# A two-layer encoder trunk with seven-product MLPs: moving the operand sums of the MLP ramp to VectorE, and the loads and places of its second phase

## The chip, the core and the metric

One core of a Trainium2 chip runs the whole kernel in one launch. The metric is device time in microseconds (us), the median of several executions. Engines are named as the profile does: PE is TensorE (PEld its weight loads), DVE is VectorE, ACT is ScalarE, POOL is GpSimd, and SP is the engine whose one queue issues nearly every DMA here. [...]

## What is computed

The input is one sequence of 1024 tokens of width 1024. There are two layers, each a mixer (attention in the first, gated linear attention in the second) and then an MLP, both with a norm ahead and a residual:

```
def sq_relu_mlp(h, w_in, w_out):
    return jnp.square(jax.nn.relu(h @ w_in)) @ w_out

for i in range(DEPTH):                      # DEPTH = 2
    hn = rmsnorm(h, norm_mix[i])
    h = h + (attention_mixer if i == 0 else gla_mixer)(hn, ...)
    h = h + sq_relu_mlp(rmsnorm(h, norm_mlp[i]), mlp_w_in[i], mlp_w_out[i])
return rmsnorm(h, final_norm)
```

`w_in` is 1024 x 4096 and `w_out` 4096 x 1024, all in float32. Everything the change touches lies in the MLP: the step from the mixer's output projection into `h @ w_in` (here the ramp), and the step from there to `@ w_out` (here the junction).

## The kernel before

Activations are held transposed, as tiles of 128 features x 512 tokens: `h[m][half]`, m = 0 to 7. Every matrix product is made of three matmuls of 128x512 (`mm_into`, L462 to L464): each float32 operand is split into a high part, cast on ACT (L97: `xh`, `wh`, `hh`), and a low part, the remainder, subtracted on DVE (L98: `xl`, `wl`, `hl`), and the products high-high, high-low and low-high are added in PSUM.

`layer_rest` (L750) is the second half of a layer. It first projects the mixer's output, adds the residual (L799), stores the result as `hm_dram`, and sums squares for the norm. `mid_norm` (L773) turns the sums of one half of the tokens into a factor `rm`: `SumSquares.rms` splits the sums into two parts (`sqh`, `sql`) and adds over the partitions with two matmuls against a matrix of ones (L161, L162), and `newton` (L125) takes the inverse root on ACT and DVE. `normed` (L776, L778) scales an `h` tile by it in place.

The MLP uses seven products P1 to P7 in place of eight, of operands that are sums and differences of quarters of the activations. With left and right half of the tokens (second index 0 and 1) and upper and lower half of the features (tiles 0 to 3 and 4 to 7): P1 and P2 use the quarters `h[k][0]` and `h[4+k][0]`; P5 uses T1 = `h[k][1] - h[k][0]` (L822); P6 uses T2 = `h[4+k][1]` - T1 (L830, tile `t2`); P7 uses T3 = `h[4+k][1] - h[k][1]` (L836, on POOL); P3 uses B22 = `h[4+k][1]`; P4 uses T4 = `h[4+k][0]` - T2 (L832, on POOL). Each operand is four tiles, and each tile is split (`xsplit`, L768).

**Phase 1** (`mlp_in`) runs 8 groups of hidden features, 7 products each, 24 matmuls per product, in the order of the list `steps` (L582): P1, P2 of group 0 and of group 1, then P5, P6, P7, P3, P4 of group 0, the same five of group 1, then all seven of each later group. A product's PSUM banks are drained by a copy on ACT (L554, tiles `s1`, `s5`, `s2`) or an add on DVE (L557); two banks with tag a and two with tag b are in turn added to by several products (P6, P7 and P4 go on in the banks of P1, P3 in those of P5). Outputs go to `hid_dram` (L530). The drained tiles of all but the first `s1` come from the pool `hid` (L845), opened after the pools `hp` (the `h` tiles) and `scratch` have closed, so a `hid` tile lies where an `h` tile lay, and its first writer waits for the last reader of that one.

**Phase 2** (`mlp_out`) runs 4 groups x 7 products x 2. Its operands are loaded from `hid_dram` into `hst` (L601, 3 buffers of 512 KB), and split into `hh` and `hl`. Its weights go to `raw`, `raw2` (6 buffers). The residual `h` is reloaded from `hm_dram` (L868, 16 loads of 256 KB) and needed only when the first outputs are drained.

Order: the tile framework's scheduler emits each engine's instructions in program order, but for blocks in `tc.high_priority(offset=-n)`, which it puts back by n; `LATER` = 150 is that number for T3, B22 and T4. Each engine then runs its list strictly in order. All loads and stores stand in SP's one list. Pools opened after others have closed take their memory.

Of the kernel before, what the change touches and what calls it, by code (L numbers as in the profile page):

```python
# [23 lines left out]
F32 = mybir.dt.float32  # L24
F32R = mybir.dt.float32r
AF = mybir.ActivationFunctionType
ALU = mybir.AluOpType
# [4 lines left out]
P = 128  # L32
# [9 lines left out]
NCH = S // P  # L42
LEAD = 22
LAG = 3
LATER = 150


C_MIX0, C_MLP0, C_MIX1, C_MLP1, C_FIN, C_QA, C_QB, C_KA, C_KB, C_OUT, NCOL = 0, 8, 16, 24, 32, 40, 41, 42, 43, 44, 46
# [2 lines left out]
def trunk_kernel(tc, xT, wqk, wv, wo, win0, wout0, gqk, gv, gvz, gr, gate, gwo, win1, wout1, cols, rope, cmat, yT):  # L51
    nc = tc.nc

    def pool_of(stack, name, bufs=1, side=None):
        return stack.enter_context(tc.tile_pool(name=name, bufs=bufs, side=side, reuse_waits="tile"))

    with ExitStack() as top:
# [35 lines left out]
        def bank(tag):  # L93
            return psum.tile([P, HN], F32, tag=tag, name="ps_" + tag, bufs=PS_BUFS[tag])
# [27 lines left out]
        def halves(n):  # L122
            return [[None, None] for _ in range(n)]
# [14 lines left out]
        class SumSquares:  # L138
# [15 lines left out]
                split(ah, al, self.acc)  # L154
                self.acc = ah, al

            def total(self, mat, tag="c"):
                if not isinstance(self.acc, tuple):
                    self.parts()
                ps = bank(tag)  # L160
                nc.tensor.matmul(ps, mat, self.acc[0], start=True, stop=False)  # L161
                nc.tensor.matmul(ps, mat, self.acc[1], start=False, stop=True)  # L162
                return ps

            def rms(self, n, out=None):

                return newton(self.total(ones), n, out)

        def gain_split(h, g, xh, xl, k, half, sums=None):

# [337 lines left out]
        def mlp_in(win, x, hx, hid, hid_dram):  # L508
# [71 lines left out]

            rest = ("P5", "P6", "P7", "P3", "P4")
            steps = [(g, p) for g in (0, 1) for p in ("P1", "P2")] + [(g, p) for g in (0, 1) for p in rest]  # L582
            steps += [(g, p) for g in range(2, ngr) for p in ("P1", "P2") + rest]
            return steps, begin, prep, run, combine, reload

# [164 lines left out]
        def layer_rest(w, src, o, gcol, win, wout, last, ahead, begun):  # L750
# [4 lines left out]
            with ExitStack() as ph:  # L755
                env.raw = Turns((wraw, 2), (pool_of(ph, "mraw", 4), 4))
                with ExitStack() as one:
# [4 lines left out]
                    env.tmp = pool_of(scratch, "tmpr", side="right")  # L762
                    big2 = pool_of(one, "big2", 8)
                    ht = halves(KT)
                    x = [([None] * 4, [None] * 4) for _ in range(7)]
                    r = [None, None]

                    def xsplit(what, k, t, pool):  # L768
                        x[what][0][k] = pool.tile([P, HN], F32R, tag="hi", name="xh")
                        x[what][1][k] = pool.tile([P, HN], F32R, tag="lo", name="xl")  # L770
                        split(x[what][0][k], x[what][1][k], t)

                    def mid_norm(half, sums):  # L773
                        r[half] = sums.rms(D, wpool.tile([P, HN], F32, tag="ro", name="rm", bufs=2))

                    def normed(k, half):  # L776
                        t = ht[k][half]
# [7 lines left out]
                    for half in range(2):  # L785
                        sums = SumSquares(nc.vector if half else nc.gpsimd)
                        for m in range(KT):
# [7 lines left out]
                            xr = hx.tile([P, HN], F32, tag="hx", name="xr")  # L795
                            nc.sync.dma_start(out=xr, in_=src[m][:, HALF[half]])
                            ps = begun.pop(0) if begun else proj("b" if m % 4 == 0 else "a", wm, o, half)
                            h = ht[m][half] = hp.tile([P, HN], F32, name=f"h{m}_{half}")
                            nc.vector.tensor_tensor(out=h, in0=ps, in1=xr, op=ALU.add)  # L799
                            sums.add(h)  # L800
                            nc.sync.dma_start(out=hm_dram[m][:, HALF[half]], in_=h)
# [23 lines left out]
                        run(*next(ramp))  # L825
                    prep(*next(weights_ahead))
                    reload()
                    for k in range(4):
                        t2 = env.tmp.tile([P, HN], F32, tag="sq", name="t2", bufs=2)
                        nc.vector.tensor_tensor(out=t2, in0=normed(4 + k, 1), in1=ht[k][0], op=ALU.subtract)  # L830
                        xsplit(T2, k, t2, big)
                        nc.gpsimd.tensor_tensor(out=ht[4 + k][0], in0=ht[4 + k][0], in1=t2, op=ALU.subtract)  # L832
                    prep(*next(weights_ahead))
                    with tc.high_priority(offset=-LATER):
                        for k in range(4):
                            nc.gpsimd.tensor_tensor(out=ht[k][1], in0=ht[4 + k][1], in1=ht[k][1], op=ALU.subtract)  # L836
                            xsplit(T3, k, ht[k][1], big)
                        for k in range(4):
                            xsplit(B22, k, ht[4 + k][1], big)
                        scratch.close()  # L840
                        big3 = pool_of(one, "big3", 4)
                        for k in range(4):
                            xsplit(T4, k, ht[4 + k][0], big3)
                    mid.close()
# [6 lines left out]
                            begin(g + 1) if g else None  # L851
                        run(g, p)
                env.tmp = pool_of(ph, "tmp2", side="right")
                raw2 = pool_of(ph, "raw2", 6)
                hst = pool_of(ph, "hst", 3)
                hp = pool_of(ph, "hacc", side="right")
                ht = halves(KT)
                for half in range(2):
# [4 lines left out]
                begin(0)  # L863
                for st in steps[:2]:
                    load(*st)
                for row, half in ((0, 0), (0, 1), (4, 1), (4, 0)):
                    for m in range(row, row + 4):
                        nc.sync.dma_start(out=ht[m][half], in_=hm_dram[m][:, HALF[half]])  # L868
                prep(*steps[0])
                for n, st in enumerate(steps):  # L870
                    if n + 2 < len(steps):
                        load(*steps[n + 2])
                    if n + 1 < len(steps):
                        prep(*steps[n + 1])
                    if st[1:] == ("P6", 0):
                        begin(st[0] + 1)
                    run(*st)
# [375 lines left out]
```

## Time and profile before

| | |
|---|---|
| median of 3 executions | 2418.49 us (2416.34 to 2419.13) |
| the profiled execution: its own time | 2420.54 us |
| span of its records | 2418.8 us |
| PE busy | 2318.6 us (96%) |
| DVE / ACT / POOL busy | 1791.2 (74%) / 1346.6 (56%) / 365.7 (15%) us |
| mean granted clock | 0.983 |

The profile is read from PE outward. PE is busy nearly all the time, so the first question is where it is not: the 40 slices of the page show it below nine tenths in a few only. The table of waits for such a stretch says which operand ended PE's idle time, the timeline of PE shows each pause and the distance between matmul starts after it (0.23 us at the full clock, 0.43 us at half), and the timelines of DVE, ACT, POOL and SP in the same stretch say what the producer of that operand did in the meantime.

### The profile page before, as it was taken

How to read it: one execution, taken by the hardware profiler on the slowest of the kernel's cores; microseconds unless marked ns; L12 is line 12 of the kernel's file. 1: busy time of each engine (PE TensorE's matmuls, PEld its weight loads, DVE VectorE, ACT ScalarE, POOL GpSimd, SP SyncE). 2: the span in 40 equal slices, each digit the busy share in tenths (PEclk: the TensorE clock that was granted, in tenths of full speed). 3: DMA queues.
4: the chain of work that ended last, by engine and by line, in shares of the span. 5: the costliest groups of instructions: out<-in, count | busy, mean ns of one | idle time of the engine just before them, and what ended most of it. 6: DMA issues, size and time to landing. Idle time of an engine off the chain costs nothing. (4 is left out here: it accounts for less than half of the span.)

```text
span 2418.8 us, 29927 instructions
## 1 busy us (share of the span) xinstructions
PE 2318.6 (96%) x10710; PEld 1907.9 (79%) x10710; DVE 1791.2 (74%) x2488; ACT 1346.6 (56%) x2388; POOL 365.7 (15%) x283
## 2 busy tenths in 40 slices
PE   8889999999979999899999999999979999899997
PEld 6777777777868888788888889888858888788885
DVE  8989999985876565788776766666785655787775
ACT  7458888884445555533344766664455555443343
POOL 2444444443020000000012000000120000000003
PEclk9999999999989999999999999999989999999999
DMA  5341212105344555844522121116515545855422
GB/s 175 129 147 53 53 27 53 27 14 177 120 139 163 164 174 199 315 163 157 165 96 78 46 72 62 44 70 224 181 70 187 174 157 187 292 200 186 155 86 70
DMA packets 157797, 317.51 MB, mean 131 GB/s; under 512 B 15048, under 2 KB 17872, under 8 KB 157520
## 3 DMA queue, kind: packets, MB, share of 16 engines
q1 hardware_dynamic: 157648, 315.60, 38.9%
q8 instruction: 84, 1.38, 0.2%
q14 instruction: 65, 0.53, 0.1%
HBM read 223.20 MB, written 92.27 MB: 130 GB/s over the span
## 5 line engine op out<-in xcount | busy, mean ns | idle before, releaser
L98 DVE TENSOR_TENSOR wl<-raw,wh 128x1024 fp32r<-128x1024 f32 x293 | 363.0, 1239 | 207.5 <-ACT wh L97 205.8
L97 ACT CAST wh<-raw 128x1024 fp32r<-128x1024 f32 x293 | 307.1, 1048 | 317.6 <-PE ps_a L463 128.6
L97 ACT CAST hh<-hst 128x512 fp32r<-128x512 f32 x224 | 134.4, 617 | 268.8 <-PE ps_a L464 128.5
L148 POOL TENSOR_TENSOR sq<-sq 128x512 f32<-128x512 f32 x35 | 54.4, 1555 | 1273.6 <-ACT sq L146 709.7
L462 PE MATMUL ps_a<-xh,wh 128*128 128x512 f32 x512 | 203.4, 398 | 8.9 <-ACT s L554 8.9
L397 POOL TENSOR_TENSOR pl<-p,ph 128x512 fp32r<-128x512 f32 x128 | 181.5, 1418 | 199.1 <-ACT p L394 130.6
L98 DVE TENSOR_TENSOR hl<-hst,hh 128x512 fp32r<-128x512 f32 x224 | 153.5, 704 | 75.3 <-ACT hh L97 74.3
L464 PE MATMUL ps_a<-xh,wl 128*128 128x512 f32 x512 | 202.8, 396 | 5.6 <-DVE wl L98 5.6
L462 PE MATMUL ps_a<-hh,wh 128*128 128x512 f32 x512 | 200.6, 393 | 7.7 <-ACT hh L97 7.7
L463 PE MATMUL ps_a<-xl,wh 128*128 128x512 f32 x512 | 203.1, 397 | 2.0 <-DVE xl L98 2.0
L463 PE MATMUL ps_a<-hl,wh 128*128 128x512 f32 x512 | 201.2, 393 | 1.1 <-DVE hl L98 1.1
L464 PE MATMUL ps_a<-hh,wl 128*128 128x512 f32 x512 | 200.4, 391 | 0.0
L274 DVE TENSOR_REDUCE mx<-ps_b 128x1 f32<-128x512 f32 x256 | 169.5, 683 | 12.6 <-PE ps_b L273 10.2
L393 ACT ACTIVATE ph<-ps_a 128x512 fp32r<-128x512 f32 x248 | 148.2, 598 | 29.8 <-PE ps_a L387 27.5
L462 PE MATMUL ps_b<-xh,wh 128*128 128x512 f32 x384 | 150.4, 392 | 8.9 <-ACT s L554 6.7
L394 ACT ACTIVATE p<-ps_a 128x512 f32<-128x512 f32 x256 | 152.3, 597 | 1.0 <-POOL pl L397 0.2
L463 PE MATMUL ps_b<-xl,wh 128*128 128x512 f32 x384 | 150.3, 391 | 0.0
L464 PE MATMUL ps_b<-xh,wl 128*128 128x512 f32 x384 | 149.5, 389 | 0.0
L502 ACT ACTIVATE s<-s 128x512 f32<-128x512 f32 x96 | 60.7, 632 | 129.0 <-DVE s L557 129.0
L462 PEld LDWEIGHTS ps_a<-xh,wh 128*128 128x128 f32 x512 | 97.9, 192 | 31.5 <-ACT s L554 9.9
L464 PEld LDWEIGHTS ps_a<-xh,wl 128*128 128x128 f32 x512 | 98.1, 192 | 26.9 <-DVE wl L98 6.4
L462 PEld LDWEIGHTS ps_a<-hh,wh 128*128 128x128 f32 x512 | 96.7, 189 | 28.5 <-ACT hh L97 8.5
(275 smaller groups left out, 6043.4 us busy)
## 6 DMA issues: line engine op xcount, KB each, us to landing
raw<-in_win_dram SPq DMA_DIRECT2D x80, 512.0 KB, 3.8
raw<-in_wout_dram SPq DMA_DIRECT2D x80, 512.0 KB, 3.4
hst<-hid_dramFalse SPq DMA_DIRECT2D x56, 512.0 KB, 4.2
hst<-hid_dramTrue SPq DMA_DIRECT2D x56, 512.0 KB, 4.8
q<-q_dram SPq DMA_DIRECT2D x96, 128.0 KB, 2.9
hid_dramFalse<-s SPq DMA_DIRECT2D x48, 256.0 KB, 2.5
hid_dramFalse<-t SPq DMA_DIRECT2D x48, 256.0 KB, 3.2
hid_dramTrue<-s SPq DMA_DIRECT2D x48, 256.0 KB, 2.0
```

The source lines that it names most:

```text
L97: nc.scalar.copy(out=hi, in_=src)
L98: (leng or nc.vector).tensor_tensor(out=lo, in0=src, in1=hi.bitcast(F32), op=ALU.subtract)
L148: self.eng.tensor_tensor(out=sq, in0=self.acc, in1=sq, op=ALU.add)
L274: nc.vector.tensor_reduce(out=mx[h][:, half * 8 + c : half * 8 + c + 1], in_=ps, axis=AX.X, op=ALU.max, negate=True)
L393: nc.scalar.activation(out=phh, in_=ps, func=AF.Exp)
L394: nc.scalar.activation(out=p, in_=ps, func=AF.Exp)
L397: (nc.vector if c % 2 == 0 else nc.gpsimd).tensor_tensor(out=pll, in0=p, in1=phh.bitcast(F32), op=ALU.subtract)
L462: nc.tensor.matmul(ps, wh, xh, start=start and i == 0, stop=False, skip_group_check=not start)
L463: nc.tensor.matmul(ps, wh, xl, start=False, stop=False, skip_group_check=not start)
L464: nc.tensor.matmul(ps, wl, xh, start=False, stop=i == len(parts) - 1, skip_group_check=not start)
L502: nc.scalar.activation(out=t, in_=src, func=AF.Relu)
```

## The change

- **Ramp.** The differences T3 and T4 move from POOL to DVE, T4 behind T3 and B22 by larger offsets (`LATER` becomes 40, and the three blocks stand at 1, 2 and 4 times it). `t2` is kept in four buffers, since T4 now reads it later.
- **Norm of the second half.** The sums are added over the partitions by one float32 matmul against ones, without the split.
- **Order of the first groups.** After P3 of group 0 come P5 and P6 of group 1, then P4 of group 0, then P7, P3, P4 of group 1.
- **Places.** The `h` tiles are allocated ahead, in an order written out in `at_slot`, so that the first `hid` tiles lie on other `h` tiles than before.
- **Phase 2.** `raw2` keeps 4 buffers, and 2 more (`raw3`) are opened behind `hst`, so that `hst` lies two buffers further forward. The residual loads are issued in four parts, in turn with steps 0, 1, 3 and 5.

```diff
-LATER = 150
+LATER = 40
...
-            def total(self, mat, tag="c"):
+            def total(self, mat, tag="c", whole=False):
+                if whole:
+                    ps = bank(tag)
+                    nc.tensor.matmul(ps, ones_f, self.acc, start=True, stop=True)
+                    return ps
...
+            steps = steps[:8] + [(1, "P5"), (1, "P6"), (0, "P4")] + steps[11:]
...
+                    at_slot = [(0, 0)] + [(4 + k, 1) for k in range(3, -1, -1)] + [(k, 1) for k in range(3, -1, -1)]
+                    at_slot += [(4 + k, 0) for k in range(3, -1, -1)] + [(k, 0) for k in range(3, 0, -1)]
+                    for m, half in at_slot:
+                        ht[m][half] = hp.tile([P, HN], F32, name=f"h{m}_{half}")
...
-                        r[half] = sums.rms(D, wpool.tile([P, HN], F32, tag="ro", name="rm", bufs=2))
+                        r[half] = sums.rms(D, whole=half == 1, out=wpool.tile([P, HN], F32, tag="ro", name="rm", bufs=2))
...
+                    t2s = []
                     for k in range(4):
-                        t2 = env.tmp.tile([P, HN], F32, tag="sq", name="t2", bufs=2)
+                        t2 = env.tmp.tile([P, HN], F32, tag="sq" if k < 2 else "t2", name="t2", bufs=2)
+                        t2s.append(t2)
                         nc.vector.tensor_tensor(out=t2, in0=normed(4 + k, 1), in1=ht[k][0], op=ALU.subtract)
                         xsplit(T2, k, t2, big)
-                        nc.gpsimd.tensor_tensor(out=ht[4 + k][0], in0=ht[4 + k][0], in1=t2, op=ALU.subtract)
                     prep(*next(weights_ahead))
                     with tc.high_priority(offset=-LATER):
                         for k in range(4):
-                            nc.gpsimd.tensor_tensor(out=ht[k][1], in0=ht[4 + k][1], in1=ht[k][1], op=ALU.subtract)
+                            nc.vector.tensor_tensor(out=ht[k][1], in0=ht[4 + k][1], in1=ht[k][1], op=ALU.subtract)
                             xsplit(T3, k, ht[k][1], big)
+                    with tc.high_priority(offset=-2 * LATER):
                         for k in range(4):
                             xsplit(B22, k, ht[4 + k][1], big)
-                        scratch.close()
-                        big3 = pool_of(one, "big3", 4)
+                    with tc.high_priority(offset=-4 * LATER):
+                        for k in range(4):
+                            nc.vector.tensor_tensor(out=ht[4 + k][0], in0=ht[4 + k][0], in1=t2s[k], op=ALU.subtract)
+                    scratch.close()
+                    big3 = pool_of(one, "big3", 4)
+                    with tc.high_priority(offset=-4 * LATER):
                         for k in range(4):
                             xsplit(T4, k, ht[4 + k][0], big3)
...
-                raw2 = pool_of(ph, "raw2", 6)
+                raw2 = pool_of(ph, "raw2", 4)
                 hst = pool_of(ph, "hst", 3)
+                raw2 = Turns((raw2, 4), (pool_of(ph, "raw3", 2), 2))
...
-                for row, half in ((0, 0), (0, 1), (4, 1), (4, 0)):
-                    for m in range(row, row + 4):
-                        nc.sync.dma_start(out=ht[m][half], in_=hm_dram[m][:, HALF[half]])
                 prep(*steps[0])
+                rows = {0: (0, 0), 1: (0, 1), 3: (4, 1), 5: (4, 0)}
                 for n, st in enumerate(steps):
+                    if n in rows:
+                        row, half = rows[n]
+                        for m in range(row, row + 4):
+                            nc.sync.dma_start(out=ht[m][half], in_=hm_dram[m][:, HALF[half]])
```

Three places show what moves in the engines' lists (numbers in names tell buffers apart; the lines of the changed kernel are four to twenty-one higher).

ACT in the first layer's ramp. The casts of the four T4 tiles (`h4_0` to `h7_0`), and behind them the drains of P5 and P6 of group 0 to `s5` and `s2`, before:

```order
L97 CAST wh_7180<-raw_7012 128x1024
L97 CAST xh_7094<-h4_0_6320 128x512
L97 CAST xh_7098<-h5_0_6359 128x512
L97 CAST xh_7102<-h6_0_6398 128x512
L97 CAST xh_7106<-h7_0_6437 128x512
L554 COPY s5_7132<-ps_b_7118 128x512
L554 COPY s5_7146<-ps_b_7119 128x512
L554 COPY s2_7164<-ps_a_6848 128x512
```

and now:

```order
L97 CAST xh_7077<-h7_1_6201 128x512
L97 CAST xh_7089<-h4_0_6212 128x512
L97 CAST xh_7093<-h5_0_6211 128x512
L97 CAST xh_7097<-h6_0_6210 128x512
L97 CAST xh_7101<-h7_0_6209 128x512
L558 COPY s5_7127<-ps_b_7113 128x512
L558 COPY s5_7141<-ps_b_7114 128x512
L558 COPY s2_7159<-ps_a_6843 128x512
```

The drains stand where they stood, behind the casts of T4; the tiles that those casts read were written by POOL and are now written by DVE.

DVE in the same stretch, the splits of the last operands (`h4_1` to `h7_1` are B22, `h4_0` to `h7_0` T4; `raw` are sums of weights), before:

```order
L98 TENSOR_TENSOR xl_7079<-h5_1_6715,xh_7078 128x512
L486 TENSOR_TENSOR raw_6798<-raw_6798,raw_6796 128x1024
L98 TENSOR_TENSOR xl_7083<-h6_1_6778,xh_7082 128x512
L98 TENSOR_TENSOR xl_7087<-h7_1_6827,xh_7086 128x512
L98 TENSOR_TENSOR xl_7095<-h4_0_6320,xh_7094 128x512
L98 TENSOR_TENSOR xl_7099<-h5_0_6359,xh_7098 128x512
```

and now:

```order
L98 TENSOR_TENSOR xl_7070<-h5_1_6203,xh_7069 128x512
L98 TENSOR_TENSOR xl_7074<-h6_1_6202,xh_7073 128x512
L98 TENSOR_TENSOR xl_7078<-h7_1_6201,xh_7077 128x512
L853 TENSOR_TENSOR h4_0_6212<-h4_0_6212,t2_7013 128x512
L853 TENSOR_TENSOR h5_0_6211<-h5_0_6211,t2_7020 128x512
L853 TENSOR_TENSOR h6_0_6210<-h6_0_6210,t2_7027 128x512
L853 TENSOR_TENSOR h7_0_6209<-h7_0_6209,t2_7034 128x512
L98 TENSOR_TENSOR xl_7090<-h4_0_6212,xh_7089 128x512
```

The four T4 differences stand between the splits of B22 and those of T4; the four of T3 stand likewise ahead of the splits of T3.

SP at the first layer's junction, the loads of phase 2's operands (`hst`) among the stores of the last group of phase 1 (`s`, `t1`, `t2`, `h21`, `t4`), before:

```order
L530 DMA hid_dramFalse_6183<-t1_9134 128x512
L601 DMA hst_9228<-hid_dramFalse_6183 128x2x512
L530 DMA hid_dramFalse_6183<-t2_9137 128x512
L530 DMA hid_dramFalse_6183<-s2_9058 128x512
L530 DMA hid_dramFalse_6183<-h21_9154 128x512
L530 DMA hid_dramFalse_6183<-t4_9158 128x512
L530 DMA hid_dramFalse_6183<-h21_9173 128x512
L530 DMA hid_dramFalse_6183<-t4_9177 128x512
L601 DMA hst_9230<-hid_dramFalse_6183 128x2x512
L601 DMA hst_9260<-hid_dramFalse_6183 128x2x512
L868 DMA h0_0_9196<-hm_dramFalse_6184 128x512
L868 DMA h1_0_9197<-hm_dramFalse_6184 128x512
```

and now:

```order
L534 DMA hid_dramFalse_6183<-s1_8949 128x512
L481 DMA raw_9216<-in_wout0_dram 128x2x512
L481 DMA raw_9222<-in_wout0_dram 128x2x512
L481 DMA raw_9224<-in_wout0_dram 128x2x512
L606 DMA hst_9226<-hid_dramFalse_6183 128x2x512
L606 DMA hst_9228<-hid_dramFalse_6183 128x2x512
L606 DMA hst_9246<-hid_dramFalse_6183 128x2x512
L481 DMA raw_9386<-in_wout0_dram 128x2x512
L606 DMA hst_9292<-hid_dramFalse_6183 128x2x512
L534 DMA hid_dramFalse_6183<-s5_9007 128x512
L606 DMA hst_9334<-hid_dramFalse_6183 128x2x512
L534 DMA hid_dramFalse_6183<-s5_9021 128x512
```

The first three `hst` loads now stand ahead of the last group's stores of `s5`, right behind loads of weights; before, the first stood behind the last group's `t1` and the next two behind all its stores, directly ahead of the residual loads.

## Rows read from the trace of the kernel before

**Rows 1.** PE's waits, 560 to 740 us: for what; total, times, longest.

```profile
PE ps_a L462 <- ACT s L554: 4.4, 1, 4.4
```

**Rows 2.** PE's timeline in layer 0's ramp: start, length, operation, idle time before and releaser.

```profile
671.57 0.39 PE L464 MATMUL ps_b<-xh,wl 128*128 128x512 f32 x1
...
697.20 0.80 PE L462 MATMUL ps_a<-xh,wh 128*128 128x512 f32 x1 [4.44 <-ACT s L554]
...
700.53 0.40 PE L464 MATMUL ps_a<-xh,wl 128*128 128x512 f32 x1
```

**Rows 3.** DVE's timeline in the same ramp.

```profile
655.42 0.68 DVE L135 SCALAR_TENSOR_TENSOR rm<-rs_t,rs_r 128x512 f32<-128x512 f32 x1
...
656.62 1.41 DVE L778 SCALAR_TENSOR_TENSOR h<-h,gneg,rm 128x512 f32<-128x512 f32 x2
...
667.78 2.90 DVE L830 TENSOR_TENSOR t<-h,h 128x512 f32<-128x512 f32 x2
...
676.96 2.29 DVE L98 TENSOR_TENSOR wl<-raw,wh 128x1024 fp32r<-128x1024 f32 x1
...
684.28 1.21 DVE L98 TENSOR_TENSOR wl<-raw,wh 128x1024 fp32r<-128x1024 f32 x1
...
694.70 3.69 DVE L98 TENSOR_TENSOR xl<-h,xh 128x512 fp32r<-128x512 f32 x6
```

**Rows 4.** POOL's timeline in the same ramp, first and last of its eight differences.

```profile
666.15 3.98 POOL L836 TENSOR_TENSOR h<-h,h 128x512 f32<-128x512 f32 x2 [60.16 <-DVE h L778]
...
681.68 2.13 POOL L832 TENSOR_TENSOR h<-h,t 128x512 f32<-128x512 f32 x1 [1.29 <-DVE t L830]
```

**Rows 5.** ACT's timeline in the same ramp, the drains to `s5` and `s2`.

```profile
696.08 0.59 ACT L554 COPY s<-ps_b 128x512 f32<-128x512 f32 x1 [4.96 <-DVE xl L98]
696.56 1.08 ACT L554 COPY s<-ps_a 128x512 f32<-128x512 f32 x2
```

**Rows 6.** DVE's timeline in layer 1's ramp.

```profile
1796.45 1.22 DVE L98 TENSOR_TENSOR wl<-raw,wh 128x1024 fp32r<-128x1024 f32 x1 [1.98 <-ACT wh L97]
```

**Rows 7.** PE's timeline at layer 0's junction, then at layer 1's.

```profile
970.23 0.39 PE L464 MATMUL ps_a<-xh,wl 128*128 128x512 f32 x1
974.93 1.22 PE L462 MATMUL ps_a<-hh,wh 128*128 128x512 f32 x2 [4.31 <-ACT hh L97]
...
995.87 0.50 PE L462 MATMUL ps_b<-hh,wh 128*128 128x512 f32 x1 [1.68 <-ACT hh L97]
...
1000.70 0.40 PE L463 MATMUL ps_b<-hl,wh 128*128 128x512 f32 x1
...
2078.43 0.39 PE L464 MATMUL ps_a<-xh,wl 128*128 128x512 f32 x1
...
2110.51 0.40 PE L462 MATMUL ps_c<-hh,wh 128*128 128x512 f32 x1
```

**Rows 8.** Busy time by stretch: length, each engine (instructions), PEclk, DMA share, GB/s.

```profile
970.00:980.00 10.00, 5.69 (x14) 3.81 (x13) 6.69 (x9) 5.01 (x8) 0.00 (x0) 0.66 0.93 326
```

**Rows 9.** SP's timeline at layer 0's junction: DMA issues, merged.

```profile
946.00 11.34 SPq L477 DMA_DIRECT2D raw<-in_wout_dram  x7
...
970.07 0.43 SPq L601 DMA_DIRECT2D hst<-hid_dramFalse  x1
...
975.92 0.95 SPq L601 DMA_DIRECT2D hst<-hid_dramFalse  x2
976.97 11.79 SPq L868 DMA_DIRECT2D h<-hm_dramFalse  x16
989.47 1.41 SPq L601 DMA_DIRECT2D hst<-hid_dramFalse  x3
```

**Rows 10.** The timeline of layer 0's second norm, ACT.

```profile
649.45 0.62 ACT L97 CAST sqh<-sq 128x512 fp32r<-128x512 f32 x1 [1.36 <-DVE sq L148]
...
651.57 0.69 ACT L129 ACTIVATE rs_r<-ps_c,epst 128x512 f32<-128x512 f32 x1 [1.01 <-PE ps_c L162]
```

**Rows 11.** The source line of another float32 matmul against ones: duration in ns.

```profile
L724 PE MATMUL ps_a<-sq,ones_f x4: 379/431/484, 2399.0 to 2406.6; 128*128 128x256 f32 x4
```

More of the change, by code (lines that the diff above doesn't have):

```diff
@@ L163, in total, with rms @@
                 return ps
-            def rms(self, n, out=None):
-                return newton(self.total(ones), n, out)
+            def rms(self, n, out=None, whole=False):
+                return newton(self.total(ones, whole=whole), n, out)
         def gain_split(h, g, xh, xl, k, half, sums=None):
@@ L797, in layer_rest @@
                             ps = begun.pop(0) if begun else proj("b" if m % 4 == 0 else "a", wm, o, half)
-                            h = ht[m][half] = hp.tile([P, HN], F32, name=f"h{m}_{half}")
+                            h = ht[m][half]
                             nc.vector.tensor_tensor(out=h, in0=ps, in1=xr, op=ALU.add)
```

## The prediction

> **What bounds the kernel now.** PE is busy for 96% of the span, so a change can only gain where PE is not. Its waits in the stretch of the first MLP's ramp are led by one for ACT, the drain of a bank [rows 1]; PE's timeline there gives the loss [rows 2]: from 671.57 to 700.53 us, the first start at full pitch after it, 28.96 us pass for 47 matmul starts. At the pitch of 0.2267 us that PE keeps outside (0.39 us records, starts 0.22 to 0.23 apart), 47 starts take 10.65. So 18.3 us go there, as pauses and as matmuls at the half clock behind them. The reader is to see who holds PE up: DVE [rows 3] works without a gap from 655.42 until the six splits that end at 698.39, 43.0 us; its instructions take about twice their usual time exactly while POOL works [rows 4] on its eight differences, 666.15 to 683.81. A pair of differences takes 2.90 there, where six splits of the same size take 3.69 afterwards (0.60 each, and 0.09 at the end); a `wl` of 1024 columns takes 2.29 and later 1.21. ACT drains P5 and P6 only at 696.08 and 696.56 [rows 5], 4.96 us idle before, released by DVE's `xl`; P7 starts on the drained bank at 697.20. Layer 1 shows the same, with one more wait of DVE, 1.98 us at 1796.45, for a cast that waits for PE [rows 6].
>
> The second place is the junction [rows 7]. In layer 0, 83 starts between 970.23 and 1000.70 take 30.47 us in place of 18.82: 11.65 lost. In layer 1, 88 starts between 2078.43 and 2110.51 take 32.08 in place of 19.95: 12.13 lost. The pauses are only part of it (4.31 and 1.68 in layer 0); the rest is the half clock after each: in the first ten microseconds PE was granted 0.66, and DMA was 0.93 busy [rows 8]. ACT's `hh` casts are what PE waits for, and those wait for `hst`: issued at 970.07 and 975.92, then three more only behind sixteen residual loads, at 989.47 [rows 9]. ACT and DVE were not full there. So the cause is the time of issue.
>
> **The norm and the front of the ramp.** Between the squared sums and the root lie a cast (649.45), two matmuls and the split's low part; the root starts at 651.57, 2.12 us after the cast [rows 10]. One float32 matmul takes their place. A float32 matmul against ones with 256 columns left records of 379 to 484 ns [rows 11]; for 512 columns I take 0.9 us, bounded by 0.45 (as two of the present ones) and 1.9 (four such records at their longest). The root then starts about 0.9 earlier (1.6 to 0.2). PE pays about 0.4 more per layer than for the pair; a part of that it idled. In DVE's new list `rm` stands ahead of a `wl`, and one drain (0.60) stands behind the first two `normed` instead of ahead. So the first `normed`, at 656.62 [rows 3], comes to about 655.1.
>
> **The differences on DVE.** From that `normed` to the last T4 difference, DVE's new list holds 53 instructions: nine of 1024 columns at 1.13, eight `normed` at 0.66 (a pair's 1.41 less its end, halved), 36 of 512 columns at 0.60: 10.2 + 5.3 + 21.6 = 37.1 us. That takes the lengths of undisturbed stretches, since POOL has nothing left to do there; I add 0.7 for hand-overs with ACT, whose casts alternate with these splits. End: 692.9. This is the balance of the part: eight more instructions cost 4.8, the contention that goes gives 7.7 (43.0 less the 35.3 that the same instructions take undisturbed).
>
> What is late next is the same drain. ACT's drains of P5 and P6 stand behind the four casts of T4 in both lists. Before, the first of them waited on top of that for a split of B22 to release its place; this wait is gone by the new places. Now the casts wait for the T4 differences on DVE. The last cast ends about 0.6 after the last difference; the third drain, which P7's bank needs, ends some 1.7 after that: P7 at 695.2, against 697.20. **Gain in layer 0: 2.0**. P5 and P6 themselves now run without stops and end near 680.4, as their operands come earlier; but that shortens no path, since PE then stands still for some 14 us in one piece. The half clock after it costs what it costs now (697.20 to 700.53). In **layer 1** the 1.98 us of DVE go too, because P6 has finished before that cast is asked for: **gain 4.0**. The new order of P5(1), P6(1), P4(0) behind it feeds PE from operands that are ready; P4's splits end 2.4 us after the differences, P4 comes 16 us after P7. I price it at nothing; cover gone would cost the 2.4. Weight loads for the group sums must land by 681.8; the reload is issued near 676, so that slack is only about 1.5 us, priced into the range with 1 us per layer.
>
> [...]
>
> **The junction.** The first three `hst` loads move ahead of the last group's stores, behind three weight loads, and wait for nothing but the queue, since their memory is no longer held until phase 1 ends. They are issued near 947, where seven weight loads stand now [rows 9]. Those took 11.34 us for seven, 1.62 each; the three weight loads and three `hst` at that rate land at 956 to 958.8. Then six casts and six low parts, 0.6 each on two engines that were 0.50 and 0.67 busy [rows 8], are done near 963; with the first weight of phase 2 (`wl`) that is 7 to 8 us ahead of PE's last matmul of phase 1 at 970.23. The following `hst` loads wait for a slot to be split, not for phase 1, and the residual loads come behind them: the third step's operands, which now arrive at 995.87, would be there before 970. What hides the edit is thus DMA time between 947 and 970, which is free for it because the residual loads (16 of 256 KB, 11.79 us) move to the other side. New waits: SP's queue waits at three points for a slot; the stores of the last group and later weights stand behind, none needed before phase 2's later steps. On ACT and DVE the splits stand ahead of the last group's drains; these would be late only if `hst` landed after about 959. The residual is needed when the first output is drained, 60 starts behind 970.5 (near 984); its first four loads are issued when the sixth `hst` has its slot, before 972, and take some 3 us at the rate above. I leave 0.25 per junction for the first weight. **Gain: 11.4 and 11.9.**
>
> **Sum.** 2.0 + 4.0 + 11.4 + 11.9 = 29.3. The profiled execution goes from 2420.54 to 2391.2. It stood 2.05 above the median of the runs, so the median goes from 2418.49 to 2389.2. The own range of this case is 2384 to 2395 (1 us for each ramp's weights, 1.5 for the norm's estimate, 2 for the half clock).
>
> **Rivals.**
> 1. *The junction closes by half.* The `hst` loads run between weight loads while the DMA engines are 0.9 busy, and each slot waits for splits; if the second three come late, the second pause remains. For it: sixteen loads of half their size take 11.79 us when the queue is full [rows 9]. Against it: 23 us of time before they are needed. Price: half of 23.3, so 2400.9.
> 2. *DVE's slowness is not POOL's doing.* If it comes from other traffic of the same time, the 7.7 stay, and P7 comes 5.7 late in each layer instead of 2.0 early; with the eight added ones slow as well (0.8 more each), 12 late. 2404.6 to 2417. Against it: all slow rows lie within POOL's 17.7 us, none behind them.
> [...]
> 4. *The splits hold up phase 1: slower than before.* The `hh` casts stand on ACT ahead of the last group's squares. If `hst` landed only when it does now (ahead of PE's start at 974.93, [rows 7]), those squares, P3, P4 and PE would wait for it: from a landing at 959 on, each microsecond costs one per layer. It takes 14.7 per layer to eat the whole gain, a landing after about 974; one at 978 would cost 38: 2389.2 + 38 = 2427. The new issue places speak against it.
> 5. *The loads stay late.* If a slot's memory is still released only at the end of phase 1, the junction keeps its loss, and only the ramps' 6.0 and little of the rest come: 2412.5.
>
> **Chances.** Forecast 0.62, rival 1 0.15, rival 2 0.07, rival 3 0.07, rival 4 0.03, rival 5 0.06. The likeliest gives 2389. The range takes in the forecast, rival 1 and the near parts of rivals 2 and 3: 2379 to 2406. A measurement of this kernel can tell about 0.2% (4.8 us) from no change: faster by more 0.92 (all of the first three, and some of rival 5), within 0.05, slower 0.03.
>
> **What would show it.** In the profile after: POOL idle in the ramp, DVE's instructions there at 0.69 and 1.21 throughout, its T4 differences ending near 693; PE busy without pauses through P6, then one pause of about 14 us that ends with P7 near 695, released by ACT's drain; in layer 1 no idle time of DVE ahead of a `wl`. At the junction `hst` issued near 947, the wait for `hh` gone from PE's table, granted clock near 1 in all its stretches. P7 later than 697 would refute the DVE part; a `hh` wait at either junction, the other.

## The result, and the profile after

The changed kernel takes 2392.52 us (median of 5 executions, 2390.56 to 2392.84), beside 2418.71 of the kernel before (5 executions, 2416.34 to 2425.6): ratio 0.9888, 95% interval 0.9876 to 0.9899. The profiled execution went from 2420.54 to 2392.76, 27.8 us less, where 29.3 were predicted.

First the page: its busy line, and the 40 slices of PE and its granted clock. The granted clock (`PEclk`) is the share of full TensorE speed that the profile shows as granted in a stretch: in the kernel after it is 1.00 from 698.50 to 705.00 us, where matmul starts are 0.23 us apart, and 0.50 from 1787.00 to 1790.00, where they are 0.43 apart; the second is called half clock here.

```profile
PE 2302.1 (96%) x10710; PEld 1899.9 (79%) x10710; DVE 1781.9 (75%) x2502; ACT 1346.5 (56%) x2386; POOL 335.8 (14%) x267
...
PE   8889999999979999999999999999979999999996
...
PEclk9989999999989999999999999999989999999998
```

PE is busy for 16.5 us less than before, since fewer matmuls run at half clock (mean granted clock 0.987, 0.983 before), and idle for 11.5 us less. Two dips remain between head and tail, one slice in each layer: the ramps. The table of PE's waits in layer 0's ramp (560 to 740 us; for what: total, times, longest) has one row in place of those led by [rows 1], and PE's timeline (start, length, operation, idle time before it and what ended it) shows that one pause in place of [rows 2]:

```profile
PE ps_b L466 <- ACT s L558: 13.4, 1, 13.4
```

```profile
680.38 0.39 PE L468 MATMUL ps_a<-xh,wl 128*128 128x512 f32 x1
694.19 0.80 PE L466 MATMUL ps_b<-xh,wh 128*128 128x512 f32 x1 [13.43 <-ACT s L558]
...
695.21 0.75 PE L466 MATMUL ps_a<-xh,wh 128*128 128x512 f32 x1
...
698.50 0.40 PE L468 MATMUL ps_a<-xh,wl 128*128 128x512 f32 x1
```

P5 and P6 run without a stop; their last matmul starts at 680.38. Then PE stands still until ACT drains. Two matmuls of P3 (on `ps_b`, P5's banks) go ahead, and P7 begins at 695.21 (697.20 before). ACT's timeline, beside [rows 5], tells what the drain stands behind:

```profile
684.45 1.13 ACT L97 CAST xh<-h 128x512 fp32r<-128x512 f32 x2
691.23 2.42 ACT L97 CAST xh<-h 128x512 fp32r<-128x512 f32 x4 [5.65 <-DVE h L853]
693.56 1.07 ACT L558 COPY s<-ps_b 128x512 f32<-128x512 f32 x2
694.52 1.09 ACT L558 COPY s<-ps_a 128x512 f32<-128x512 f32 x2
```

DVE's timeline, beside [rows 3], tells what those casts wait for:

```profile
655.65 1.41 DVE L787 SCALAR_TENSOR_TENSOR h<-h,gneg,rm 128x512 f32<-128x512 f32 x2
...
668.01 0.68 DVE L841 TENSOR_TENSOR t<-h,h 128x512 f32<-128x512 f32 x1
...
681.82 1.22 DVE L487 TENSOR_TENSOR raw<-raw 128x1024 f32<-128x1024 f32 x1
...
688.71 1.89 DVE L98 TENSOR_TENSOR xl<-h,xh 128x512 fp32r<-128x512 f32 x3
690.51 2.49 DVE L853 TENSOR_TENSOR h<-h,t 128x512 f32<-128x512 f32 x4
```

DVE's instructions have their undisturbed lengths throughout (0.68 for a difference, 1.22 for 1024 columns). The banks to be drained were complete by 680.8 and ACT idled 5.65 us, but ACT's next instruction was a cast of T4, and DVE made the T4 differences last, behind four sums of weights (L487 is the first of them) and the splits of B22, of which the row at 688.71 holds the last three.

The junction of layer 0 in PE's timeline, beside [rows 7]:

```profile
968.11 0.39 PE L468 MATMUL ps_a<-xh,wl 128*128 128x512 f32 x1
968.34 0.39 PE L466 MATMUL ps_a<-hh,wh 128*128 128x512 f32 x1
...
973.53 0.50 PE L466 MATMUL ps_a<-hh,wh 128*128 128x512 f32 x1 [0.95 <-ACT h L506]
...
988.62 0.39 PE L466 MATMUL ps_c<-hh,wh 128*128 128x512 f32 x1
```

and in SP's (issues, merged), beside [rows 9]:

```profile
943.87 1.58 SPq L481 DMA_DIRECT2D raw<-in_wout_dram  x3
945.49 2.18 SPq L606 DMA_DIRECT2D hst<-hid_dramFalse  x3
...
967.17 0.41 SPq L606 DMA_DIRECT2D hst<-hid_dramFalse  x1
...
976.99 8.68 SPq L888 DMA_DIRECT2D h<-hm_dramFalse  x12
```

The first `hst` loads go out at 945.49, the first residual load 31 us later. PE goes from phase 1 into phase 2 with no pause for `hh`; the granted clock is 1.00 in each ten microseconds from 970 to 1000. The first of the three, in the columns of [rows 8], where it was 0.66:

```profile
970.00:980.00 10.00, 9.05 (x40) 7.17 (x39) 10.00 (x13) 5.48 (x9) 0.00 (x0) 1.00 0.97 325
```

What is left is one pause for ACT, at 973.53.

### The profile page after: what moved, and what is told of

It is laid out like the page before. It is cut to its first block, busy times and chain, and to the rows that moved or that the text cites. A ratio compares the mean times of both kernels' runs of the same rounds, so it can differ in the third digit from the quotient of the medians.

```text
span 2390.8 us, 29877 instructions
## 1 busy us (share of the span) xinstructions
PE 2302.1 (96%) x10710; PEld 1899.9 (79%) x10710; DVE 1781.9 (75%) x2502; ACT 1346.5 (56%) x2386; POOL 335.8 (14%) x267
## 5 line engine op out<-in xcount | busy, mean ns | idle before, releaser
L277 PE MATMUL ps_b<-k,q 128*128 128x512 f32 x256 | 105.8, 415 | 9.4 <-DVE mx L278 9.4
```

The lines of the kernel that those rows point to most:

```text
L277: nc.tensor.matmul(ps, q1[h][:, c * P : c * P + P], kst[h // 4][0][:, HALF[half]], start=True, stop=True)
```

## The experiments

Differences are against the kernel after unless it says otherwise. Each was timed beside runs of the kernel before; the ratios are to those.

**Each half alone.** `ramp_only` undoes the edits of phase 2; `junction_only` is the kernel before with these edits alone.

```diff
-                raw2 = pool_of(ph, "raw2", 4)
+                raw2 = pool_of(ph, "raw2", 6)
                 hst = pool_of(ph, "hst", 3)
-                raw2 = Turns((raw2, 4), (pool_of(ph, "raw3", 2), 2))
...
+                for row, half in ((0, 0), (0, 1), (4, 1), (4, 0)):
+                    for m in range(row, row + 4):
+                        nc.sync.dma_start(out=ht[m][half], in_=hm_dram[m][:, HALF[half]])
```

> Phase 2's places and residual loads as before, the ramp as changed. If the two parts add up (my account of the two traces: ramps 2.1 and 5.1 us, junctions 10.4 and 11.4), this stands some 7 us under the kernel before, near 2411.5, and both junctions show the waits for hh again (4.3 and 1.7 us in layer 0). Rival: the ramp's gain needs the junction's (it shifts the same loads) or is a matter of the clock alone; then it is within 3 us of the kernel before, 2416 to 2419.

> The ramp as before, phase 2's places and residual loads as changed. If the parts add up, 21 us under the kernel before, near 2397.5, with the ramp's waits of 4.4, 3.5 and 2.8 us as before and no wait for hh at the junction. Rival: with the old list of phase 1, whose places release later, the hst loads move less; then a hh wait stays, and the time is 2402 to 2410.

`ramp_only` took 2410.89 us (ratio 0.9965, 0.9952 to 0.9978), `junction_only` 2398.06 (0.9910, 0.9895 to 0.9925). The two gains, 8.8 and 21.6 us by the ratios' own references, make 30 together, beside 26 (medians) to 28 (profiled executions) of the whole: they add, within what these runs can tell. Most of the change's worth is the junction.

**Within the junction: the places, or the residual?** `old_places2` gives `raw2` its 6 buffers ahead of `hst` again and keeps the residual in four parts; `old_residual` keeps the new places and issues the sixteen residual loads in a row.

> Only the places of phase 2 undone (raw2 of six buffers ahead of hst); the residual loads stay in four parts. Theory: the place carries the junction, because an hst load in the old place waits until phase 1 has ended whatever the residual loads do. Then the first pause of 4.3 us and the half clock behind it come back in both layers and part of the second, together 12 to 20 us: 2405 to 2412. Rival: the residual loads in parts carry it, since they stood ahead of the third to fifth hst; then only the first pause's part comes back, below 8 us, or less: 2393 to 2400.

> Only the residual loads undone (all sixteen in one row ahead of the first step), the new places stay. Theory: by then six hst loads have been issued, so the row of sixteen holds up only weights, by some 3 us, which have more slack than that: 2391 to 2395. Rival, residual loads carry the second pause: a hh or wh wait near 990 comes back, 5 us per layer: 2399 to 2405.

`old_places2` took 2404.89 us (0.9937, 0.9922 to 0.9952), 12 more than after. In its timeline of PE the first pause is back, at its old length:

```profile
972.40 1.22 PE L466 MATMUL ps_a<-hh,wh 128*128 128x512 f32 x2 [4.31 <-ACT hh L97]
```

Its timeline of SP shows `hst` issued when phase 1 ends:

```profile
967.73 0.43 SPq L606 DMA_DIRECT2D hst<-hid_dramFalse  x1
...
973.60 0.94 SPq L606 DMA_DIRECT2D hst<-hid_dramFalse  x2
974.59 5.18 SPq L887 DMA_DIRECT2D h<-hm_dramFalse  x8
980.90 1.07 SPq L606 DMA_DIRECT2D hst<-hid_dramFalse  x2
```

The second pause stays away, because the parted residual lets `hst` in between. `old_residual` took 2391.65 (0.9884, 0.9868 to 0.9901): no difference. So the places carry the junction: without any of the edits 2410.89 (`ramp_only`), with the places alone 2391.65, 19.2 less; with the parted residual alone 2404.89, 6.0 less. Beside the new places the parted residual does nothing.

**Within the ramp: who made the gain?** `pool_diffs` leaves the eight differences on POOL. `old_slots` is `pool_diffs` with the `h` tiles also in the order in which they are made, as before.

```diff
-   nc.vector.tensor_tensor(out=ht[k][1], in0=ht[4 + k][1], in1=ht[k][1], op=ALU.subtract)
+   nc.gpsimd.tensor_tensor(out=ht[k][1], in0=ht[4 + k][1], in1=ht[k][1], op=ALU.subtract)
...
-   nc.vector.tensor_tensor(out=ht[4 + k][0], in0=ht[4 + k][0], in1=t2s[k], op=ALU.subtract)
+   nc.gpsimd.tensor_tensor(out=ht[4 + k][0], in0=ht[4 + k][0], in1=t2s[k], op=ALU.subtract)
```

```diff
-   at_slot = [(0, 0)] + [(4 + k, 1) for k in range(3, -1, -1)] + [(k, 1) for k in range(3, -1, -1)]
-   at_slot += [(4 + k, 0) for k in range(3, -1, -1)] + [(k, 0) for k in range(3, 0, -1)]
+   at_slot = [(m, half) for half in range(2) for m in range(KT)]
```

> The changed kernel with its eight differences per layer on POOL again, all else as changed. Theory (POOL's work slows DVE's by 7.7 us, and the path is ACT's list: the drains of P5 and P6 stand behind a weight cast that waits for DVE's sum of weights and behind the casts of T4): DVE's pairs take 2.9 again in place of 1.28, its sum of weights comes 7.7 later but 2.4 earlier for the four differences that it no longer does; T4 no longer waits for DVE. P7 starts near 692, 3 us earlier than in the changed kernel: 2384 to 2389. First rival, DVE's slowness has another cause: DVE is as fast as in the changed kernel or as slow in both; with it fast, P7 starts near 687: 2374 to 2380. Second rival, the move to VectorE is what made the ramp faster: P7 comes later than 695.2, time 2395 to 2405.

> The earlier kernel with the T3 and T4 differences on GpSimd (2385.3 us), with one more part undone: the tiles of h lie in the order in which they are made, as before the change, not in the order of release. In ScalarE's list the second of the four early drains then waits for VectorE again, as in the kernel before; everything else in the lists stays. Theory A (what the ramp gained came from these places): that drain waits for the last splits of B22, which stood at 694.4 to 698.0 us in the kernel it is compared with; P7 starts at 696 to 698 us of the first layer instead of 692.1, 4 to 6 us later in each layer, 2393 to 2397 us. Rival B (the places do not matter; the gain came from the norm, the order of the steps and the later due times): 2384 to 2387 us.

`pool_diffs` took 2385.33 us (0.9854, 0.9839 to 0.9868): 7 us **less** than the changed kernel. The move to DVE, the first item of the change, is a loss. In the two profiled executions 2.9 and 3.1 us of it arise in the two ramps and 1.3 near the end, where the granted clock differs (1.00 against 0.83 after) though the edit lies elsewhere (last section). `old_slots` took 2397.38 (0.9911, 0.9893 to 0.9929), 12 more than `pool_diffs`, just above what the theory of the places gave; in the profiled executions 5.4 and 5.2 of it arise in the ramps. ACT's timeline of `pool_diffs`:

```profile
689.98 1.13 ACT L97 CAST xh<-h 128x512 fp32r<-128x512 f32 x2
691.01 1.06 ACT L558 COPY s<-ps_b 128x512 f32<-128x512 f32 x2
691.97 1.09 ACT L558 COPY s<-ps_a 128x512 f32<-128x512 f32 x2
```

and of `old_slots`:

```profile
692.01 0.58 ACT L558 COPY s<-ps_b 128x512 f32<-128x512 f32 x1
696.81 0.59 ACT L558 COPY s<-ps_b 128x512 f32<-128x512 f32 x1 [4.22 <-DVE xl L98]
697.29 1.08 ACT L558 COPY s<-ps_a 128x512 f32<-128x512 f32 x2
```

In `old_slots` the second drain waits 4.22 us for DVE's last splits, as in [rows 5]: its tile lies where a B22 tile lies. With `at_slot` it waits for nothing. In `pool_diffs` DVE is as slow as before while POOL works, and P6 has its pauses again, but P7 starts at 692.62 instead of 695.21. A row of DVE's timeline, and one of PE's:

```profile
676.69 2.28 DVE L98 TENSOR_TENSOR wl<-raw,wh 128x1024 fp32r<-128x1024 f32 x1
```

```profile
692.62 0.79 PE L466 MATMUL ps_a<-xh,wh 128*128 128x512 f32 x1
```

The steps close: `junction_only` 2398.06; with the ramp's other edits, but neither places nor move, 2397.38; with the places 2385.33; with the move 2392.52.

One corner is missing: the move with the old places was not run. The rows of the kernel after suggest that it would come near 2392.5 too. There the last split of B22 ends at 690.6, ahead of the T4 casts that the drains stand behind, so a drain in an old place would find it free. By this estimate the move, taken first, would bring some 5 us, and the places nothing on top of it. So, by these rows, each of the two takes away the wait for B22's splits; shown is that the places without the move do it better than both together.

**Why the move costs: ACT's list, or DVE's load?** `late_dve` keeps the differences on DVE and only puts the preparation of the weights for P5 of group 1 (four sums of weights, and the split of the first) back, behind T4. `best` does the same, by 5 times `LATER`, with the differences on POOL.

```diff
-                            prep(*nxt)
+                            with tc.high_priority(offset=-10 * LATER if nxt == (1, "P5") else 0):
+                                prep(*nxt)
```

> The kernel after with one difference: the preparation behind P5 (weight sums on VectorE, their casts on ScalarE) is emitted later, so that VectorE makes the T4 differences before these sums. The differences stay on VectorE. Theory A (the list of ScalarE in order: T4 casts, then one cast of the sums, then the drains): T4 differences end about 4.5 us earlier, the cast of the sums is then what the drains stand behind, P7 at 691 to 692 us of the first layer instead of 695.2, 2385 to 2388 us. Rival B (the differences on VectorE cost time only because they share the engine's rate with other work, not by their place in the list): P7 where it is, 2391 to 2394 us.

> The kernel after, with two differences: the subtractions and absolute values of the T3 and T4 tiles run on GpSimd again (as in the earlier run with that one part undone, 2385.3 us), and the preparation of the second layer of the pair that follows P5 (its weight sums and casts) is emitted later, so that in ScalarE's list the T4 casts and the drains of the early tiles come ahead of the cast of the sums. Theory A (ScalarE takes its list in order, and the pause before P3 and P7 lasts until its drains): the drains start about 3 us earlier than in that run, P7 starts at about 689.7 us of the first layer instead of 692.1, some 2.4 us less per layer, 2380.5 us (2378 to 2384). Rival B (the pause is set by the end of the T4 differences alone, whatever stands between them and the drains): no difference from that run, 2384 to 2387.

`late_dve` took 2383.29 us (0.9854, 0.9839 to 0.9869), 9 less than after and less than expected. The last two of its four T4 differences in DVE's timeline:

```profile
685.37 1.29 DVE L853 TENSOR_TENSOR h<-h,t 128x512 f32<-128x512 f32 x2
```

ACT's timeline behind them:

```profile
687.87 1.04 ACT L97 CAST wh<-raw 128x1024 fp32r<-128x1024 f32 x1 [0.56 <-DVE raw L487]
688.82 1.07 ACT L558 COPY s<-ps_b 128x512 f32<-128x512 f32 x2
```

and PE's:

```profile
689.45 0.80 PE L466 MATMUL ps_b<-xh,wh 128*128 128x512 f32 x1 [9.36 <-ACT s L558]
...
690.47 0.75 PE L466 MATMUL ps_a<-xh,wh 128*128 128x512 f32 x1
```

P7 starts 4.74 us earlier than after (PE was 0.65 ahead already when it came to the ramp), with the same instructions on DVE in another order, all at undisturbed lengths. Over the whole ramps the two traces differ by 4.5 us in layer 0 and 3.7 in layer 1. So the move costs by its place in the list: the drains stand behind the T4 casts, these behind the T4 differences, and these stood behind the sums. The drains now wait for one cast of a sum, which the expectation put later than it came, since the sum itself went ahead of the last splits.

`best` took 2386.15 (0.9867, 0.9850 to 0.9883): not better than `pool_diffs`. The expectation's first step held: P7 at 689.89, as forecast. Its result did not. PE's timeline has a pause behind that which `pool_diffs` does not have:

```profile
689.89 0.50 PE L466 MATMUL ps_a<-xh,wh 128*128 128x512 f32 x1 [0.23 <-ACT s L558]
...
702.54 0.47 PE L466 MATMUL ps_b<-xh,wh 128*128 128x512 f32 x1 [1.93 <-DVE s L561]
```

and DVE's timeline shows what stands ahead of the add that PE waits for:

```profile
700.56 1.22 DVE L98 TENSOR_TENSOR wl<-raw,wh 128x1024 fp32r<-128x1024 f32 x1 [1.70 <-ACT wh L97]
701.71 0.68 DVE L561 TENSOR_TENSOR s<-ps_b,s 128x512 f32<-128x512 f32 x1
```

A split of a weight waits there for its cast on ACT, ahead of the add that empties PE's next bank, and PE's matmuls behind it are at half clock once more (0.83 granted in the ten microseconds from 700). That takes back what P7 gained (2.73): at 714 us PE is only 0.1 ahead of `pool_diffs`, and layer 1's ramp gains nothing either (1.1 us ahead before it, 1.2 behind it). The profiled execution (2383.22) is still 2.1 us faster than that of `pool_diffs`; this lead arises outside the ramps. Why it was 3 us faster than the other three (2386.1 to 2388.0), its trace alone does not tell.

**What disturbs DVE.** `pool_reads` adds eight subtractions of 128x448 on POOL to each ramp, two inputs each and into a tile that nobody reads; `pool_writes` adds one such subtraction and 32 memsets of the same tile. The output is that of the kernel after.

```diff
+                    dm = env.tmp.tile([P, 448], F32, tag="dm", name="dm")
...
+                        for _ in range(2):
+                            nc.gpsimd.tensor_tensor(out=dm, in0=ht[4 + k][1][:, :448], in1=ht[4 + k][1][:, :448], op=ALU.subtract)
```

> The changed kernel, its differences on DVE, with eight POOL subtractions of 128x448 from two SBUF operands added per layer while DVE forms T2 and T3 (their result is used by nothing). Theory: DVE's instructions with two SBUF operands slow down as before, by some 7 us per layer (eight times 0.9 us; 448 columns in place of 512), and P7 comes as much later: 2403 to 2408. [...] Rival, POOL is not the cause: 2391 to 2394.

> The same place, but POOL only writes: one subtraction and then 32 fills of the same 128x448 tile per layer. Theory: what disturbs DVE is POOL's reading, so DVE keeps 0.69 and 1.22 us: 2391 to 2394.5. Rival, any POOL work that touches SBUF disturbs DVE: its instructions get longer while the fills run, 2398 or more.

`pool_reads` took 2400.33 us (0.9921, 0.9903 to 0.9938), less than expected. POOL's timeline:

```profile
664.62 9.23 POOL L845 TENSOR_TENSOR dm<-h 128x448 f32<-128x448 f32 x6 [59.41 <-DVE h L787]
674.55 3.12 POOL L845 TENSOR_TENSOR dm<-h 128x448 f32<-128x448 f32 x2 [0.69 <-DVE h L787]
```

and three rows of DVE's in that time:

```profile
668.96 1.42 DVE L787 SCALAR_TENSOR_TENSOR h<-h,gneg,rm 128x512 f32<-128x512 f32 x1
670.30 0.68 DVE L561 TENSOR_TENSOR s<-ps_b,s 128x512 f32<-128x512 f32 x1
...
671.64 1.42 DVE L842 TENSOR_TENSOR t<-h,h 128x512 f32<-128x512 f32 x1
```

While POOL works, six of DVE's eleven instructions with two inputs from SBUF take 1.42 in place of 0.68 to 0.74, two take 0.82, and three keep their usual length; the adds with one input from PSUM stay at 0.68. Over their usual lengths DVE's rows lose 4.6 us for 12.35 us of POOL, and PE loses 5.0 us in this ramp and 3.8 in layer 1's. `pool_writes` took 2392.48 (0.9884, 0.9870 to 0.9899), the time of after, though POOL works longer:

```profile
667.48 16.90 POOL L847 MEMSET dm<- 128x448 f32 x32
```

and DVE's rows keep their lengths beside the memsets, as this one:

```profile
670.35 0.68 DVE L842 TENSOR_TENSOR t<-h,h 128x512 f32<-128x512 f32 x1
```

So in these runs POOL's subtractions, which read two SBUF tiles, lengthen DVE's instructions with two SBUF inputs (up to 1.42), and its memsets, which read none, leave them at 0.68 to 0.74. DVE does not stand still while POOL works: it loses 4.6 of the 12.35 us.

**The small parts.** `old_norm` has the split norm back, `old_steps` the old order of the first groups.

> Only the norm of the second half undone (cast, low part and two matmuls again). Theory: the first scaled tile comes some 0.9 us later and all of DVE's chain with it, P7 as much in both layers: +1.8, 2393.5 to 2395. Rival: the sum of weights that DVE forms waits for a load, so the front of the chain has slack: no difference, 2391 to 2393.

> The kernel after with the order of the first steps of the ramp as it was before (not interleaved), all places as after. Theory A (the gain of the ramp comes from the places, so that the early tiles no longer wait for VectorE): no difference that can be measured, 2391 to 2394 us. Rival B (the interleaving carries part of it): the waits of P5 and P6 of the kernel before come back in part, 1 to 2 us per layer, 2394 to 2397 us.

They took 2393.02 (0.9888, 0.9873 to 0.9902) and 2392.73 (0.9893, 0.9878 to 0.9908): neither can be told from after. The larger offsets of T3, B22 and T4 were not undone by themselves; with the norm and the order they are all that parts `old_slots` from `junction_only`, 0.7 us. In `old_norm` the first `normed` comes 1.04 us later (656.69), but P3 only 0.36 later (694.55).

## Why the prediction was right

Gains in us in the profiled executions, from the shift of the same matmuls between the two traces:

| step | predicted | measured |
|---|---|---|
| ramp, layer 0 | 2.0 | 2.5 |
| junction, layer 0 | 11.4 | 10.4 |
| ramp, layer 1 | 4.0 | 5.1 |
| junction, layer 1 | 11.9 | 11.4 |
| sum of the four | 29.3 | 29.4 |
| elsewhere | 0 | -1.6 |

The sum is as close as it is in part by luck: the two ramps gave 1.6 more than forecast, the two junctions 1.5 less, and 1.6 went elsewhere.

- **The list of DVE.** By the trace's own time, in which PE and DVE came to this ramp 0.35 us later than before (lost in the first 165 us): first `normed` 655.65 (forecast 655.1), T4 differences done at 693.0 (692.9), P6 out at 680.38 (680.4), P7 at 695.21 (695.2). Counting the new list in undisturbed lengths, 53 instructions one by one, gave this. The premise, that DVE's doubled lengths come from POOL, was shown by `pool_reads` (1.42 in place of 0.68 to 0.74). Rival 2 is out with it. No run shows the term behind the 0.07 of rival 3, which also has a part in the range: beside POOL's 15.2 us DVE lost 7.7 by the prediction's count, and in `pool_reads` 4.6 beside 12.35.
- **The norm.** The float32 matmul of 512 columns leaves two records of 0.59 to 0.70 us that overlap, 1.10 from start to end in place of the 0.9 taken. The root starts 0.5 us earlier (651.06); since the squared sum came 0.36 later (649.10, 648.74 before), the step itself is 0.87 shorter, as forecast. `old_norm` shows that the term was not worth its place in the sum.
- **The junction.** Issue, landing and the absence of the `hh` wait came as forecast; rivals 1, 4 and 5 did not occur. Mis-sized was the 0.25 left for the first weight. The remaining pause is another: P4's second drain stands on ACT behind other work, in layer 0 a fill of `zt` (1.06) and a new `hh` cast, in layer 1 an `hh` cast that waits 0.79 for its `hst` load. It cost 1.1 and 0.6. The first residual loads went out at 976.99, not before 972 as forecast; PE did not wait for them.
- **Layer 1's ramp.** PE came to it 13.2 us ahead, started P7 (1786.98) 17.7 ahead and ended phase 1 18.4 ahead: 4.5 for P7, where 4.0 was forecast (DVE's 1.98 us of [rows 6] are gone, as forecast), and 0.6 for a shorter stretch at half clock behind P7's first start (3.5 us, 4.9 before), which had no term.
- **Elsewhere.** Ahead of the first ramp the new kernel lost 0.35, between the layers 0.8 to small waits, and it escaped one half-clock stretch there (1.5 back): behind a pause of 0.73 us the kernel before ran eight matmuls 0.43 us apart from 1287.07 (0.87 granted from 1280 to 1290), and the new one, behind the same 0.73 at 1275.35, ran on at full clock (1.00 from 1272 to 1282). At the end it lost 1.4 to 1.7 (below).
- **What the prediction had no eye for.** It added up the whole ramp and got its size and its path, but gave the credit to the move: "eight more instructions cost 4.8, the contention that goes gives 7.7". That balance is right for DVE's end and says nothing of ACT's drain, which needs the T4 casts and no more of DVE's list. `old_slots` and `pool_diffs` show that the places without the move give 12 us by the medians (10.6 in the ramps of the traces) and that the move, on top of them, takes 7 back (6.0 in the ramps). Its sign for "the DVE part", P7 no later than 697, could not tell this: P7 is in time with the places alone (692.62), and late with neither (697.94 in `old_slots`). The prediction had named the released place in half a sentence, but took the drain that waited for the first one; it was the second. The first stood earlier, in ACT's timeline of the kernel before:

```profile
690.54 0.57 ACT L554 COPY s<-ps_b 128x512 f32<-128x512 f32 x1
```

Asked separately, "what if only the places were changed", this row and three drains of about half a microsecond each would have put P7 near 692.2; `pool_diffs` has it at 692.62.

Of the versions tried, `late_dve` (2383.29), `pool_diffs` (2385.33) and `best` (2386.15) beat both kernels; by their ratios the runs do not tell the three apart.

## What to carry to other kernels

When a change bundles a move with a new order and new places, cost each alone: here the places alone would have given more than the whole gain of the ramps, and the move took about half of that back. Follow the waiting engine's list upward to the first instruction that is not ready, and then ask what stands ahead of that one's producer; four sums of weights in DVE's list cost some 4 us per layer because they stood ahead of the operands that the drain stood behind. Where loads wait for memory and not for data, the order of pools is a schedule: two weight buffers opened behind the operand buffers were worth 19 us.

## What the runs showed of the hardware

The same pause did not cost the same clock. Near the end PE waits for a cast ahead of a norm matmul. PE's timeline of the kernel before:

```profile
2380.22 0.50 PE L161 MATMUL ps_a<-sqh,ones 128*128 128x512 f32 x1 [2.50 <-ACT sqh L97]
```

and of the kernel after:

```profile
2350.48 0.80 PE L165 MATMUL ps_a<-sqh,ones 128*128 128x512 f32 x1 [2.51 <-ACT sqh L97]
```

After 2.50 us of idling PE went on at full clock, after 2.51 at half: 0.83 granted in the ten microseconds from 2350, 1.00 in those from 2380 before. That was worth 1.4 to 1.7 us, about all that parts the sum of the four steps (29.4) from the result (27.8). In `pool_diffs`, `best` and `late_dve` PE's table of waits has the same pause, 2.5 us; the granted clock is 1.00 from 2340 to 2360 in the first two and 0.83 from 2340 to 2350 in the third. So in these five traces the length of the pause does not decide between full and half clock; what does, no run here separates. Two kernels that are compared by a few microseconds can differ by this alone.
